# Feed-forward input product in seven block products for eight (Strassen's method), output sums carried by DMA stores that add, in a hybrid encoder block

## Chip, core and metric

The kernel runs on one core of a Trainium2 chip. The metric is the device time of one execution in microseconds (us). Engines are named TensorE (PE in the rows; PEld is its weight load), VectorE (DVE), ScalarE (ACT), GpSimd (POOL) and SyncE (SP, which only issues DMAs).

## The reference

An encoder block on 1024 tokens of width 1024: an attention branch and a state-space branch behind one input projection, mixed by gates, then a SwiGLU feed-forward part. The change lies in the last part, but for eight rows of the conditioning vector `ada`:

```python
ada = jax.nn.silu(c) @ w_ada[l] + b_ada[l]
sh1, sc1, gt1, sh2, sc2, gt2 = jnp.split(ada[:, None, :], 6, axis=-1)
...
h = _rms(x, g_pre_ffn[l]) * (1.0 + sc2) + sh2
g, up = jnp.split(h @ w_ffn_in[l], 2, axis=-1)      # 1024 x 1024 @ 1024 x 5632
f = (jax.nn.silu(g) * up) @ w_ffn_out[l]            # 1024 x 2816 @ 2816 x 1024
x = x + gt2 * _rms(f, g_post_ffn[l])
```

## The kernel before

Everything is float32. A product is made from operands split into a high part that TensorE takes as it is and a low part that is the rest: `mm3` (lines 197 to 203) issues three matmuls for each 128x128 block of weights, high x high, high x low, low x high, on 512 columns of tokens. The split costs a copy on ScalarE and a subtraction on VectorE, for weights in `WStream.split` (line 183 and `tt`, line 66), for activations in the functions that make them.

Tokens are in two halves of 512 columns, named h = 0 and 1 (`halves`). The normalised input of the feed-forward part is `h2t[h]`, eight blocks of 128 rows each. The 2816 hidden columns are 22 pairs of a gate and an up tile of 128 columns. `ffn_in(p, hs)` (line 1599) makes, for one pair and each half, two products of 8 blocks x 3 matmuls, then Silu on ScalarE, the multiply, and the split of f into `fhi` and `flo`. `ffn_out` (line 1616) multiplies the pairs of one group by the output weights: for each m of 8 and each half, 3 matmuls a pair, and VectorE adds the result onto a running sum in SBUF, `facc` (line 1625).

`FGROUPS` (line 33) sets the groups, 4, 4, 4, 4, 3 and 3 pairs, and `units` the order: for each group its input products, then its output products. In the first and the last group the two halves are run one after the other. In the first this lets the second half's normalisation (`chain`) run beside the first half's products; in the last it lets the first half's last pass, `final` (row sums of squares, scaling, the sum with the kept `x1d`, stores), run beside the second half's input products. The second half of the last group goes in two quarters of 256 columns. `backlog`, `tick` and `drain` (line 1463) cut such side work into pieces: `prod` (line 1477) calls `tick` after every second block, which emits the next piece and the stores in `pending` (ScalarE's queue).

All instructions are in program order on each engine; waits are by semaphores. PSUM has eight buffers of 512 columns in this stage (`ps_b`). Weights come by SyncE's queue into two raw buffers of 512 KB (`wraw`) and three split ones (`whi`, `wlo`). The last eight rows of `ada` are loaded and reduced (`ada_do`, line 937) within the feed-forward stage.

## Time and profile before

| | |
|---|---|
| three runs, us | 1680.84, 1685.55, 1686.59; median 1685.55 |
| the profiled execution, us | 1684.47, span of its instructions 1682.7 |
| granted TensorE clock, mean | 0.983 of full speed |
| DMA | 189.66 MB, 113 GB/s over the span |
| feed-forward stage | about 915 us to the end |

Rows of the profile give busy times for each engine, and a row of the trace in order of time says what ended the idle time ahead of an instruction. A matmul's duration is that from its start to the end of its results; the next one starts before.

### The profile page before, as it was taken

Reading aid. Unit: us, or ns where it says so; the run is one execution under the profiler, and the core shown is the slowest. Engines: PE = TensorE matmul, PEld = TensorE weight load, DVE = VectorE, ACT = ScalarE, POOL = GpSimd, SP = SyncE. Lnnn points to the kernel's source line nnn. Section 1 sums busy time; section 2 is a strip of 40 time slices with the busy share of each in tenths; the row PEclk is TensorE's granted clock in tenths of the full one; section 3 lists DMA queues with packets and bytes.
Section 4 is the critical chain, followed back from the end, with each engine's and each line's share of the span. In section 5 each row is a group of like instructions: output and inputs, shape, how many; then the busy total and the mean of one; then the engine's idle time right before and its main releaser. Section 6 shows DMA issues by size and latency. Waiting matters only on the chain.

```text
span 1682.7 us, 19415 instructions
## 1 busy us (share of the span) xinstructions
PE 1618.4 (96%) x7454; PEld 1309.0 (78%) x7454; DVE 977.7 (58%) x1615; ACT 552.5 (33%) x743; POOL 164.0 (10%) x221
## 2 busy tenths in 40 slices
PE   6989999999899999999999999999999999999995
PEld 6878888888688677767777778888888888888874
DVE  6978898977857778854636763223223222323366
ACT  4142322223531467763334443211111121121233
POOL 0430000012220000000524200000000000000002
PEclk9899999999999999999999999999999999999998
DMA  8143333567987424202523442212111111111243
GB/s 330 63 124 100 108 103 94 157 218 221 310 244 223 104 63 101 45 14 67 196 94 107 162 135 91 73 66 79 59 63 51 50 51 50 51 41 48 80 142 129
DMA packets 90748, 189.66 MB, mean 113 GB/s; under 512 B 19992, under 2 KB 36504, under 8 KB 90656
## 3 DMA queue, kind: packets, MB, share of 16 engines
q1 hardware_dynamic: 57920, 120.62, 23.7%
q10 hardware_dynamic: 27104, 49.95, 8.6%
q0 software_dynamic: 5632, 17.86, 3.5%
q8 instruction: 58, 0.95, 0.2%
q14 instruction: 34, 0.28, 0.1%
HBM read 148.61 MB, written 39.78 MB: 112 GB/s over the span
## 4 chain that ended last, share of the span: by engine, by line
PE 65%; DVE 20%; ACT 5%; DMA 4%; issue 4%; ACTq 1%; SPq 0%; DVEq 0%; POOLq 0%
PE mm L203 17%; PE mm L202 17%; PE mm L201 17%; DVE t L66 5%; DVE wlo L66 2%; PE sc L1255 1%; PE sc L1256 1%; PE sc L1257 1%; PE pv L1281 1%; PE pv L1280 1%; PE pv L1282 1%; ACT whi L183 1%; DMA mxd<-mneg 1%; PE mx L1203 1%; DVE s L695 1%
## 5 line engine op out<-in xcount | busy, mean ns | idle before, releaser
L202 PE MATMUL mm<-mh,whi 128*128 128x512 f32 x736 | 289.3, 393 | 4.8 <-DVE mh L74 3.1
L201 PE MATMUL mm<-mh,whi 128*128 128x512 f32 x736 | 289.8, 394 | 0.8 <-ACT mh L1404 0.5
L203 PE MATMUL mm<-mh,wlo 128*128 128x512 f32 x736 | 288.7, 392 | 1.7 <-DVE wlo L66 1.6
L66 DVE TENSOR_TENSOR wlo<-wraw,whi 128x1024 fp32r<-128x1024 f32 (+1 forms) x128 | 155.8, 1235 | 80.2 <-ACT whi L183 80.1
L66 DVE TENSOR_TENSOR silu<-mm,silu 128x512 f32<-128x512 f32 x44 | 30.4, 692 | 277.4 <-PE mm L203 271.2
L183 ACT CAST whi<-wraw 128x1024 fp32r<-128x1024 f32 (+1 forms) x128 | 129.9, 1036 | 149.0 <-PE mm L202 137.0
L202 PEld LDWEIGHTS mm<-mh,whi 128*128 128x128 f32 x736 | 139.2, 189 | 38.2 <-DVE mh L74 6.6
L203 PEld LDWEIGHTS mm<-mh,wlo 128*128 128x128 f32 x736 | 139.2, 189 | 32.9 <-DVE wlo L66 4.3
L201 PEld LDWEIGHTS mm<-mh,whi 128*128 128x128 f32 x736 | 139.2, 189 | 31.1 <-ACT whi L183 0.9
L201 PE MATMUL mm<-hhi,whi 128*128 128x512 f32 x384 | 156.7, 408 | 1.5 <-ACT ev L604 1.5
L202 PE MATMUL mm<-hlo,whi 128*128 128x512 f32 x384 | 152.8, 398 | 1.4 <-DVE hlo L74 1.4
L203 PE MATMUL mm<-hhi,wlo 128*128 128x512 f32 x384 | 153.5, 400 | 0.0
L201 PE MATMUL mm<-fhi,whi 128*128 128x512 f32 x304 | 118.8, 391 | 0.0
L202 PE MATMUL mm<-flo,whi 128*128 128x512 f32 x304 | 118.5, 390 | 0.0
L203 PE MATMUL mm<-fhi,wlo 128*128 128x512 f32 x304 | 118.3, 389 | 0.0
L66 DVE TENSOR_TENSOR mr<-mm,mr 128x512 f32<-128x512 f32 (+1 forms) x88 | 56.3, 641 | 97.1 <-PE mm L203 97.0
L66 DVE TENSOR_TENSOR plo<-p,phi 128x1024 fp32r<-128x1024 f32 x64 | 78.3, 1224 | 40.0 <-ACT phi L1261 39.6
L1613 ACT CAST fhi<-silu 128x512 fp32r<-128x512 f32 x44 | 27.3, 621 | 222.2 <-DVE silu L66 222.2
L201 PEld LDWEIGHTS mm<-hhi,whi 128*128 128x128 f32 x384 | 73.3, 191 | 19.6 <-ACT ev L604 1.9
L202 PEld LDWEIGHTS mm<-hlo,whi 128*128 128x128 f32 x384 | 73.1, 190 | 18.5 <-DVE hlo L74 1.8
L1260 ACT ACTIVATE p<-sc 128x1024 f32<-128x1024 f32 x64 | 65.7, 1026 | 64.5 <-PE sc L1257 64.5
L203 PEld LDWEIGHTS mm<-hhi,wlo 128*128 128x128 f32 x384 | 73.0, 190 | 17.9 <-DVE wlo L66 0.2
(524 smaller groups left out, 2938.7 us busy)
## 6 DMA issues: line engine op xcount, KB each, us to landing
wraw<-in_wfi SPq DMA_DIRECT2D x58, 512.0 KB
wraw<-in_win SPq DMA_DIRECT2D x26, 512.0 KB
wraw<-in_wfo SPq DMA_DIRECT2D x20, 512.0 KB
gdram<-ev ACTq DMA_DIRECT2D x32, 256.0 KB
wada<-in_wada POOLq DMA_DIRECT2D x15, 512.0 KB, 4.3
wraw<-in_wmix SPq DMA_DIRECT2D x10, 512.0 KB
xT<-in_xT SPq DMA_DIRECT2D x8, 512.0 KB
pw<-in_wadk SPq DMA_DIRECT2D x8, 512.0 KB
```

Source lines behind the costliest of these rows:

```text
L66: return self.eng.tensor_tensor(o, a, b, op=op)
L183: A_.copy(hi, t)
L201: PE.matmul(ps, whi[:, c], rhi, start=first, stop=False)
L202: PE.matmul(ps, whi[:, c], rlo, start=False, stop=False)
L203: PE.matmul(ps, wlo[:, c], rhi, start=False, stop=last)
L695: V.tensor_tensor_scan(t[64:P, 511::-1], r[64:P, ::-1], z[i][64:P, ::-1], 0.0, op0=ALU.mult, op1=ALU.add)
L1203: PE.matmul(pieces[j], qt["qhi"][b][0:96, t * P:(t + 1) * P], qt["khi"][b][0:96, halves[j]], start=True, stop=True)
L1255: PE.matmul(ps[:, c], kh[0:97, kc], qh[0:97, c], start=True, stop=False)
L1256: PE.matmul(ps[:, c], kh[0:96, kc], ql[0:96, c], start=False, stop=False)
L1257: PE.matmul(ps[:, c], kl[0:96, kc], qh[0:96, c], start=False, stop=True)
L1260: A_.activation(p, ps, AF.Exp)
L1613: A_.copy(fh[:, c], t)
```

## The change

Groups are now 4, 2, 2, 2, 2, 2, 2, 2 and 4 pairs. Group 0 goes as before, one half of the tokens after the other. For the 18 pairs from the fifth on, `pair7` makes the gate and up tile for all 1024 tokens by Strassen's method in Winograd's form: weights and activations are cut into 2 x 2 blocks (gate and up by halves of the contraction; halves of the contraction by halves of the tokens), and seven products of 4 blocks x 3 matmuls replace eight. Sums of activation blocks, T1 to T4, are made once (`tops_12`, `tops_4`, `tops_3`); sums of weight blocks, S1 to S4, for each pair on GpSimd (class `Blocks`, which also loads the weights by GpSimd's queue and splits them, three blocks ahead). VectorE combines the seven results. In group order, each `ffn_out` result is copied by ScalarE into one of four buffers (`fio`) and sent to DRAM (`fd`): group 0 by a plain store on SyncE's queue, groups 1 to 7 by stores on GpSimd's queue that add to what is there. The last group loads the sums back and adds them on VectorE. The last group no longer runs its input products by halves; for the first half, `final` now adds x on GpSimd in all eight tiles. The last eight rows of `ada` are loaded and reduced in the last steps of attention. The order of the output weights in DRAM follows the groups.

```diff
-FGROUPS = [4, 4, 4, 4, 3, 3]
+FGROUPS = [4, 2, 2, 2, 2, 2, 2, 2, 4]
+AHEAD = 3
...
         if i in ATT_ADA:
-            ada_do(1)
-            ada_load(min(1, len(ada_rest) - 8), gp, "wada", 1)
+            ada_do()
+        if 51 <= i < 62:
+            if len(ada_live) > 1 or i >= 59:
+                ada_do(1)
+            ada_load(1, ap, "wada", 2, SY)
...
+    for hs in ((0,), (1,)):
+        units += [("in", p, hs) for p in range(FGROUPS[0])] + [("out", 0, hs)]
...
+    fd = dram.tile([2, KD, P, HF], F32, name="fd")
...
+    def ft_put(p, c, t):
+        fh, fl = ft[p]
+        A_.copy(fh[:, c], t)
+        tt(fl[:, c], t, fh[:, c].bitcast(F32), ALU.subtract)
...
+        if g == last:
+            r = facc[h][:, m, c0:c0 + n]
+            tt(r, ps, fio.pop(0), ALU.add)
+            return r
+        r = f_tile()
+        A_.copy(r, ps)
+        if g:
+            G.dma_start(fd[h, m], r, accum_op=ALU.add)
         else:
-            tt(r, ps, r, ALU.add)
-        return r
+            SY.dma_start(fd[h, m], r)
...
+        def load(self, n=1):
+            for _ in range(n):
+                if self.loads:
+                    t = wp.tile([P, D], F32, name="wraw", tag="wraw", bufs=2)
+                    src = self.loads.pop(0)
+                    G.dma_start(t.rearrange("p (m c) -> p m c", m=2) if len(src.shape) == 3 else t, src)
+                    self.raw.append(t)
...
+        def split(self, src, out=None):
+            hi, lo = out or self.new(src.shape[1])
+            A_.copy(hi, src)
+            tt(lo, src, hi.bitcast(F32), ALU.subtract)
+            self.done.append((hi, lo))
...
+                    g, u = self.g, self.u = self.raw.pop(0), self.raw.pop(0)
+                    self.split(g[:, lo])
+                    self.s1, self.s2 = half_tile(c2, "xk", NXK), half_tile(c2, "xk", NXK)
+                    G.tensor_tensor(self.s1, u[:, lo], u[:, hi], op=ALU.add)
+                    G.tensor_tensor(self.s2, self.s1, g[:, lo], op=ALU.subtract)
+                    G.tensor_tensor(u[:, lo], g[:, lo], u[:, lo], op=ALU.subtract)
+                elif kind == "S2":
+                    self.split(self.s2)
+                elif kind == "S1":
+                    self.split(self.s1)
+                elif kind == "S3":
+                    self.split(self.u[:, lo])
+                elif kind == "A12":
+                    self.split(self.g[:, hi])
+                    G.tensor_tensor(self.g[:, hi], self.g[:, hi], self.s2, op=ALU.subtract)
+                elif kind == "A22":
+                    self.split(self.u[:, hi])
+                elif kind == "S4":
+                    self.split(self.g[:, hi])
+                    self.load(2)
+                elif kind == "O":
+                    self.split(self.raw[0][:, halves[j % 2]])
+                    if j % 2:
+                        self.raw.pop(0)
+                        self.load()
+                else:
+                    self.split(self.raw.pop(0), self.out() if j == 3 else None)
...
+        def get(self):
+            self.advance(self.got + 1 + self.ahead())
+            self.got += 1
+            return self.done.pop(0)
+
+        def ahead(self):
+
+            return AHEAD if self.got < len(self.seq) - 5 else 2
...
+    def tops_12():
+
+        for nm in ("T1", "T2"):
+            top_new(nm, mhc.tile([P, KD, HF], F32R, name=nm, tag=nm))
+        v, (h0, l0) = mos[1], h2t[0]
+        for j in range(4):
+            t1, t2 = half_tile(c2, "ht"), half_tile(c2, "sq")
+            stt(t1, v[:, j, :], sh2[:, j:j + 1], h0[:, j, :].bitcast(F32), ALU.add, ALU.subtract)
+            yield
+            tt(t1, t1, l0[:, j, :].bitcast(F32), ALU.subtract)
+            yield
+            t_split(t1, "T1", j)
+            yield
+            stt(t2, v[:, 4 + j, :], sh2[:, 4 + j:5 + j], t1, ALU.add, ALU.subtract)
+            yield
+            t_split(t2, "T2", j)
...
+    def tops_3():
+
+        v = mos[1]
+        top_new("T3", row_big(0, F32R))
+        for j in range(4):
+            t = half_tile(c2, "ht")
+            stt(t, v[:, 4 + j, :], dsh[:, j:j + 1], v[:, j, :], ALU.add, ALU.subtract)
+            t_split(t, "T3", j)
...
+    def sprod(ps, w, x):
+        hi, lo = x
+        for k in range(4):
+            mm3(ps, w, hi[:, k, :], lo[:, k, :], k, k == 0, k == 3)
+            if k % 2:
+                tick()
...
+    def pair7(p, prep):
+
+        (h0, l0), (h1, l1) = h2t[0], h2t[1]
+        b11, b21 = ((h0[:, k:k + 4, :], l0[:, k:k + 4, :]) for k in (0, 4))
+        b22 = h1[:, 4:8, :], l1[:, 4:8, :]
+        lo, hi = halves
+
+        def prod7(x):
+            ps = ps_b()
+            sprod(ps, bl.get(), x)
+            return ps
+
+        p1, u2, u3 = half_tile(c2, "ht"), half_tile(c2, "sq"), half_tile(c2, "acc1", 1)
+        gl, uh = half_tile(c2, "acc0", 1), half_tile(c2, "rs", 1)
+        A_.copy(p1, prod7(b11))
+        tt(u2, prod7(tops["T2"]), p1, ALU.add)
+        ps5 = prod7(tops["T1"])
+        prep()
+        tt(u3, prod7(tops["T3"]), u2, ALU.add)
+        tt(uh, ps5, u3, ALU.add)
+        tt(u2, ps5, u2, ALU.add)
+        tt(gl, prod7(b21), p1, ALU.add)
+        A_.activation(gl, gl, AF.Silu)
+        tt(p1, prod7(tops["T4"]), u3, ALU.add)
+        tt(gl, gl, p1, ALU.mult)
+        ft_put(p, lo, gl)
+        tt(u2, prod7(b22), u2, ALU.add)
+        A_.activation(u2, u2, AF.Silu)
+        tt(u2, u2, uh, ALU.mult)
+        ft_put(p, hi, u2)
...
-            if h and (c0 == 0 or m % 2 == 0):
+            if not h or c0 == 0 or m % 2 == 0:
...
+        big_first = g % 2 == 0
+        for n, p in enumerate(range(starts[g], starts[g + 1])):
+            if (n < 2) == big_first:
+                if n % 2 == 0:
+                    ft_big(1, p)
+            else:
+                ft_new(p)
+            pair7(p, drain if p == starts[1] else tick)
+        if g == last:
+            break
+        order = [(m, h) for m in range(KD) for h in range(2)]
+        for m, h in order:
+            if m % 2 == 0 and h == 0:
+                w = bl.get()
+            ffn_out(g, m, h, w, m % 2 * FGROUPS[g])
...
+    for h, c0, n in ((0, 0, HF), (1, 0, QF), (1, QF, QF)):
+        sq = Squares(c2, half_tile(c2, "acc0" if h == 0 else "acc1", 1)[:, 0:n], V)
+        for m in range(3):
+            f_load(h, m, c0, n)
+        for m in range(KD):
+            if h == m % 2 == 0:
+                out_w[m // 2] = bl.get()
+            if m + 3 < KD:
+                f_load(h, m + 3, c0, n)
+            r = ffn_out(last, m, h, out_w[m // 2], m % 2 * FGROUPS[last], c0, n)
+            sq.add(r)
+            A_.activation(r, r, AF.Copy, scale=gg2[:, m:m + 1])
```

What the change does to the order of instructions is shown at three places. First TensorE, where an output stage begins (`mh` are input blocks, `fhi`, `flo` and in some groups `mr` the two parts of f). Before, a group of four pairs, from its last input matmul on, with the waits of each:

```order
L203 MATMUL mm<-mh,wlo 128x512
L201 MATMUL mm<-fhi,whi 128x512 [waits Activation_49]
L202 MATMUL mm<-flo,whi 128x512
L203 MATMUL mm<-fhi,wlo 128x512 [waits DVE_49]
L201 MATMUL mm<-fhi,whi 128x512
L202 MATMUL mm<-flo,whi 128x512
L203 MATMUL mm<-fhi,wlo 128x512
L201 MATMUL mm<-fhi,whi 128x512
L202 MATMUL mm<-flo,whi 128x512
L203 MATMUL mm<-fhi,wlo 128x512
L201 MATMUL mm<-fhi,whi 128x512 [waits Activation_49]
L202 MATMUL mm<-flo,whi 128x512 [waits DVE_49]
```

Now, the group of pairs 6 and 7:

```order
L205 MATMUL mm<-mh,wlo 128x512
L203 MATMUL mm<-mr_9400,whi 128x512 [waits Activation_49]
L204 MATMUL mm<-mr_9400,whi 128x512
L205 MATMUL mm<-mr_9400,wlo 128x512 [waits DVE_49]
L203 MATMUL mm<-mr_9400,whi 128x512 [waits Activation_49]
L204 MATMUL mm<-mr_9400,whi 128x512 [waits DVE_49]
L205 MATMUL mm<-mr_9400,wlo 128x512
L203 MATMUL mm<-mr_9400,whi 128x512
L204 MATMUL mm<-mr_9400,whi 128x512
L205 MATMUL mm<-mr_9400,wlo 128x512
L203 MATMUL mm<-mr_9400,whi 128x512 [waits Activation_49]
L204 MATMUL mm<-mr_9400,whi 128x512 [waits DVE_49]
```

The waits before are for the last pair's first half, made a pair of products earlier; its second half is first read in the second tile, by the 22nd matmul. Now the second tile follows after six matmuls, and the last pair's second half, with the waits for its high and its low part, is read by the tenth and eleventh.

Second GpSimd, in the output stage of group 2; `wraw` is a raw weight buffer, `xk` a sum of weight blocks, `fd` the running sums in DRAM. Before, its queue held in the feed-forward stage eight loads of `ada` rows and the sums of the last pass. Now:

```order
L1688 DMA wraw<-in_wfi 128x1024 [waits DMASW5_49,DMASW3_49,DVE_49]
L1662 DMA fd<-fio 128x512 [waits DMASW6_49,Activation_49]
L1662 DMA fd<-fio 128x512 [waits DMASW7_49,Activation_49]
L1662 DMA fd<-fio 128x512 [waits Activation_49] x2
L1718 TENSOR_TENSOR xk<-wraw 128x512 [waits DMASW5_49]
L1719 TENSOR_TENSOR xk<-xk,wraw 128x512 [waits DMASW4_49,Pool_49]
L1720 TENSOR_TENSOR wraw<-wraw 128x512
L1662 DMA fd<-fio 128x512 [waits Activation_49] x4
L1662 DMA fd<-fio 128x512 [waits DMASW6_49,Activation_49]
L1662 DMA fd<-fio 128x512 [waits DMASW7_49,Activation_49]
```

A weight load, four stores that add, three sums that need the load, and the other stores stand in one queue.

Third ScalarE, between the first and the second quarter of the last half. Before, the squares (`sq`, `acc`) and scalings followed each other:

```order
L1498 ACTIVATE sq<-mr 128x256 [waits DVE_49]
L1708 ACTIVATE mr<-mr,gg_7139 128x256 [waits Activation_49]
L1494 ACTIVATE acc_12347<-mr 128x256 [waits DVE_49,PE_49]
L1708 ACTIVATE mr<-mr,gg_7139 128x256 [waits Activation_49]
L1498 ACTIVATE sq<-mr 128x256 [waits DVE_49]
L1708 ACTIVATE mr<-mr,gg_7139 128x256 [waits Activation_49]
L1498 ACTIVATE sq<-mr 128x256 [waits DVE_49]
L1708 ACTIVATE mr<-mr,gg_7139 128x256 [waits Activation_49]
```

Now:

```order
L149 DMA out_xt<-mh 128x512 [waits DMAHW0_49,Pool_49]
L149 DMA xk<-x1d 128x512 [waits DMAHW2_49]
L149 DMA out_xt<-mh 128x512 [waits DMAHW3_49,Pool_49]
L149 DMA out_xt<-mh 128x512 [waits DMAHW5_49,Pool_49]
L149 DMA out_xt<-mh 128x512 [waits DMAHW6_49,Pool_49]
L1499 ACTIVATE acc_13162<-mh 128x256 [waits DVE_49,PE_49]
L1940 ACTIVATE mh<-mh,gg_7175 128x256 [waits Activation_49]
L1503 ACTIVATE sq<-mh 128x256 [waits DVE_49]
L1940 ACTIVATE mh<-mh,gg_7175 128x256 [waits Activation_49]
```

The first half's last output stores, each waiting for GpSimd, and loads of x stand ahead of the second quarter's first square.

## Rows read from the trace of the kernel before

**Rows 1.** The page's first part: busy us (share of the span) and instructions of each engine.

```profile
PE 1618.4 (96%) x7454; PEld 1309.0 (78%) x7454; DVE 977.7 (58%) x1615; ACT 552.5 (33%) x743; POOL 164.0 (10%) x221
```

**Rows 2.** Stretches: busy us (count) per engine, granted clock, DMA share, GB/s.

```profile
1050.00:1600.00 550.00, 549.63 (x2424) 454.68 (x2423) 168.12 (x218) 103.18 (x137) 3.18 (x6) 1.00 0.18 59
...
1645.00:1666.00 21.00, 17.05 (x137) 16.39 (x135) 17.07 (x48) 14.05 (x32) 2.20 (x3) 1.00 0.39 130
1666.00:1683.00 17.00, 2.21 (x6) 1.43 (x6) 10.12 (x30) 0.00 (x0) 6.49 (x9) 0.51 0.33 109
```

**Rows 3.** Groups by shape, 1050 to 1600 us: count, busy us, mean ns, idle before.

```profile
L201 PE MATMUL mm<-mh,whi 128*128 128x512 f32 x528 | 205.4, 389 | 0.0
...
L66 DVE TENSOR_TENSOR mr<-mm,mr 128x512 f32<-128x512 f32 x68 | 47.0, 691 | 95.3 <-PE mm L203 95.3
...
L1613 ACT CAST fhi<-silu 128x512 fp32r<-128x512 f32 x33 | 20.5, 621 | 185.0 <-DVE silu L66 185.0
L1610 ACT ACTIVATE silu<-mm 128x512 f32<-128x512 f32 x33 | 19.8, 599 | 110.8 <-PE mm L203 110.8
...
L1623 ACT COPY mr<-mm 128x512 f32<-128x512 f32 x6 | 3.5, 587 | 10.0 <-PE mm L203 10.0
```

**Rows 4.** TensorE in order of time, 1641 to 1646 us: start, us, [idle before].

```profile
1641.35 0.39 PE L203 MATMUL mm<-mh,wlo 128*128 128x512 f32 x1
...
1643.24 0.38 PE L201 MATMUL mm<-fhi,wada 128*128 128x256 f32 x1 [0.79 <-ACT fhi L1613]
1643.97 0.38 PE L202 MATMUL mm<-flo,wada 128*128 128x256 f32 x1 [0.34 <-DVE flo L66]
...
1645.38 0.28 PE L201 MATMUL mm<-fhi,mh 128*128 128x256 f32 x1
1645.50 0.28 PE L202 MATMUL mm<-flo,mh 128*128 128x256 f32 x1
```

**Rows 5.** Groups by shape, whole span, GpSimd's passes of 512 columns.

```profile
L1504 POOL TENSOR_TENSOR acc<-acc,sq 128x512 f32<-128x512 f32 x28 | 40.7, 1461 | 103.7 <-ACT sq L1498 93.5 <-issue 10.0
...
L1412 POOL TENSOR_TENSOR mh<-t,mh 128x512 fp32r<-128x512 f32 x16 | 25.2, 1601 | 61.8 <-ACT mh L1404 61.8
```

**Rows 6.** GpSimd in order of time: one issue.

```profile
319.82 0.54 POOL L951 DMA_DIRECT2D er<-in_wada  x1 [1.02 <-DVE t L66]
```

**Rows 7.** DMA issues: count, KB each, us from issue to landing.

```profile
wada<-in_wada POOLq DMA_DIRECT2D x15, 512.0 KB, 4.3
...
er<-in_wada POOLq DMA_DIRECT2D x10, 256.0 KB, 3.7
...
kr<-pdram POOLq DMA_DIRECT2D x1, 512.0 KB, 11.6
...
qhi<-mxd POOLq DMA_DIRECT2D x8, 4.0 KB, 2.8
```

**Rows 8.** Groups by shape, 1645 to 1683 us, ScalarE's passes of 256 columns.

```profile
L1708 ACT ACTIVATE mr<-mr,gg 128x256 f32<-128x256 f32 x16 | 8.2, 510 | 0.5
...
L1498 ACT ACTIVATE sq<-mr 128x256 f32<-128x256 f32 x14 | 5.7, 409 | 3.5 <-DVE mr L66 3.2
```

**Rows 9.** TensorE in order of time, end of the last quarter.

```profile
1663.59 0.28 PE L203 MATMUL mm<-fhi,mh 128*128 128x256 f32 x1
1666.40 0.77 PE L245 MATMUL mm<-ones,acc 128*128 128x1 f32 x3 [2.53 <-DVE acc L1504]
```

**Rows 10.** The output tensor's instructions: ns min/median/max of a store's issue.

```profile
L147 ACTq DMA_DIRECT2D out_xt<-mr x24: 338/344/587, 1628.9 to 1677.7; - x24
```

**Rows 11.** VectorE in order of time, attention's last steps.

```profile
739.24 1.23 DVE L66 TENSOR_TENSOR plo<-p,phi 128x1024 fp32r<-128x1024 f32 x1 [1.57 <-ACT phi L1261]
742.03 1.23 DVE L66 TENSOR_TENSOR plo<-p,phi 128x1024 fp32r<-128x1024 f32 x1 [1.56 <-ACT phi L1261]
...
756.76 1.22 DVE L66 TENSOR_TENSOR rb<-rb,oraw 64x1024 f32<-64x1024 f32 x1
```

**Rows 12.** Groups by shape, whole span: one conditioning row's reduction.

```profile
L455 DVE SCALAR_TENSOR_TENSOR wada<-wada,sil 128x1024 f32<-128x1024 f32 x24 | 29.3, 1220 | 10.0 <-DMA wada<-in_wada 10.0
```

235 lines of the change are left out of this document (142 added, 93 removed).

## Prediction

> **What bounds the kernel now.** I read the busy shares first, then stretches of the feed-forward stage, then single rows at the places that the change touches. TensorE is busy 96% of the span, VectorE 58% [rows 1]. From 1050 to 1600 us, nearly all of the feed-forward stage, TensorE is never idle and runs at the full granted clock, while VectorE, ScalarE and GpSimd have much room [rows 2]. So each matmul that is left out there is worth its spacing, not its duration: the row of the group says 389 ns [rows 3], but matmuls overlap, and 2424 of them in 550 us come every 226.9 ns [rows 2]. Whatever makes TensorE wait in this stage costs in full. After 1666 us TensorE has no more products, and a chain of small steps ends the run [rows 2].
>
> **Matmuls.** 18 pairs of 128 hidden columns had 8 block products each (gate and up, two halves of the tokens, two halves of the contraction) and now have 7, each of 4 x 3 = 12 matmuls. That is 18 x 12 = 216 matmuls of 512 columns less: 216 x 0.2269 = **-49.0 us**. The last group has four pairs for three, so its second half, in two quarters, has 192 matmuls of 256 columns for 144, against 24 of 512 less. With 0.12 us each [rows 4]: 48 x 0.12 - 24 x 0.2269 = **+0.3 us**. The output product keeps its work.
>
> **Load of the other engines.** A group of two pairs now takes TensorE 14 products of 12 and 16 tiles of 6 matmuls, 14 x 2.72 + 16 x 1.36 = 59.9 us. Beside it VectorE has 18 splits and 22 other passes of 512, 40 x 0.69 = 28 us; ScalarE some 44 passes of about 0.6 us, 26 us [rows 3]; GpSimd 8 sums of 1.46 us and 24 DMA issues of 0.54 us, 25 us [rows 5, 6]. None is a bound on average, so I cost this work at nothing, and look at the places where it is in a chain.
>
> **Seams.** Seven times (groups 1 to 7) the output product starts right after the last product of a pair, and that pair's second half of f is only then made: add, Silu, multiply, copy, subtract. The last three steps are seen before: the last product's matmul starts at 1641.35, the next slot is 1641.58, and the matmul that needs the low part starts at 1643.97, 2.39 us on [rows 4]. An add of 0.69 and a Silu of 0.60 come ahead [rows 3], with handovers 3.74 us. In the changed order ten matmuls that need nothing new stand before that matmul (six of the first tile, three and one of the second): 2.27 us. The rest is a stall of 1.47 us, seven times **+10.3 us**. Before, groups of three or four pairs covered it, and only the last unit paid: 0.79 + 0.34 = 1.1 us [rows 4], which goes away, **-1.1 us**, since in the last group the whole first half of the output covers it.
>
> **The stores that add.** No accumulating DMA is in the trace, so the price is bounded. Let L be the time from its issue to its landing. It goes through GpSimd's queue, and four buffers hold the tiles. I follow one output stage, with 0 at its start. GpSimd first issues a weight load that waits for the split of the weights before it, behind the seam's chain up to its copy, 3.05 us, and takes a cast and a subtraction itself, 1.3 us [rows 3]: at 4.4 us. Four accumulates follow it, then three sums that need that load: landing 4.3 us later [rows 7], 8.7, and 3 x 1.46 more, 13.1. The fifth to eighth accumulates are issued at 13.1 to 14.7, every 0.54 us. The twelfth tile's copy waits for the eighth: 14.7 + L, copy 0.59 [rows 3], issue, L again, copy of the sixteenth: done at 15.9 + 2L. Behind it in ScalarE's queue stands the split of the fourth weight block, 1.3 us. TensorE has its output stage until 23.3 us (16 x 1.36 and the seam) and three products that are already split, to 31.5. So it doesn't wait while 15.9 + 2L + 1.3 is below 31.5: **L below 7.1 us is free**; each us beyond costs 2 us a group, 14 in all. Bounds: a plain load of this size from this queue lands in 3.7 us, and the slowest load of this queue takes 11.6 [rows 7]; lower than the plain load I exclude, since the accumulate moves the same bytes and one read more. At 11.6 the stall would be 9.0 a group, 63 us. I take 6.5: the plain 3.7, plus one more dependent round trip, for which I take the 2.8 of a 4 KB load [rows 7]. It is nearer the low end because that row is the same size, queue and engine; the 11.6 us belongs to a load that stood behind two others. So **0 us**, with 0.6 us of L to spare.
>
> The Trainium skill, "Collectives: The Full Stack", section "The bandwidth ceiling: the fold count and why AG ≠ RS ≠ AR", says that a DMA which adds is slower not for the adding but because it reads two sources through one ring. By that an accumulate would cost the plain load's data time twice; an estimate with the page's own halving gives at most 2 x 3.7 = 7.4 us, 0.6 us a group or 4 us more in the sum, 1656, and less if only the moving part doubles. No run here shows it yet.
>
> **The tail.** The first half's last pass (norm, eight multiplies, eight sums with x, eight stores) was hidden under 33 us of input products (3 pairs x 48 matmuls x 0.2269); now it runs beside the two quarters of the second half. Its eight sums have moved to GpSimd at 1.3 to 1.6 us [rows 5], and ScalarE issues its stores in order, each waiting for its sum, ahead of the second quarter's squares. The first sum can start some 11 us into the first quarter, the last ends at 11 + 8 x 1.46 = 22.7, and only then can ScalarE do 16 passes of 0.41 or 0.51 and eight stores of 0.34, 10.1 us [rows 8, 10]: its squares end near 33 us. The second quarter's products end at 23. The row sums come some 10 us after the products, for 2.8 us now (1663.59 to 1666.40) [rows 9]; of this about 2 us are given back, because the 4 us of idle TensorE between 1645 and 1666 [rows 2] lie inside the same time. I take **+5 us**, with 0 (ScalarE's passes fit between the stores) and 10 as ends.
>
> **Attention.** Eight conditioning rows are reduced in its last steps for in the feed-forward stage, where they were hidden. A step takes 2.79 us, and VectorE is idle 1.57 of it [rows 11]; a row's reduction is 1.22 us [rows 12] with two small steps behind it. It fits, but not beside the passes of the softmax's normalisation (three like the one of 1.22 us) [rows 11]: some 3.7 us late, of which the two steps of lag take most. **+2 us**; 0 to 8.
>
> The sums T1 to T4 of the activations, some 40 passes of 0.69 us on VectorE, lie beside 65 us of group 0's products of the second half, and the weight loads that follow the sixteenth accumulate have, by the same clock, some 4 us of lead: nothing. If that cover is gone, rival 3 says what it costs.
>
> **Sum.** The profiled execution took 1684.47 us; it lies 0.06% under the median of the runs shown, 1685.55. 1684.5 - 49.0 + 0.3 + 10.3 - 1.1 + 0 + 5 + 2 = **1652 us**.
>
> **Rivals.**
> 1. *Slow accumulates.* The four buffers drain slower than the stage fills them; ScalarE's copies wait for them, and the next weights' splits behind the copies. For it: the first sums on GpSimd's queue hold half of the accumulates back, and two round trips follow each other. Against: DMA is used little here, 59 GB/s [rows 2]. The other terms leave 32.5 us, 4.6 a group, so L of 9.4 us eats all of it. At 11.6 us: 1652 + 63 = **1715**, slower. With L from 7.1 to 9 the time is 1652 to 1679.
> 2. *GpSimd late.* An accumulate takes twice the issue time of a plain load, 1.08 us, and a sum the 1.60 of its slower row [rows 5]. Issues and sums ahead of the sixteenth copy then add some 3 us to the chain; less the 1.2 us to spare (2 x 0.6 us of L), 1.8 a group: 1652 + 13 = **1665**. Each engine still has room.
> 3. *The saving isn't had*, because split weights or sums come late and TensorE waits once in each pair: 18 x 2.7 = 49, one product's time per pair; **1701**. Against it: the splits run three products ahead, and the changed order has exactly 192 matmuls fewer (216 - 24).
>
> **Chances.** Forecast (1642 to 1662) 0.57; accumulates or GpSimd late by a little, still faster (1662 to 1680) 0.19; about even (within 0.3%, 5 us, what a measurement of this kernel can tell from no change) 0.07; slow accumulates or late weights, slower 0.17. So faster 0.76, same 0.07, slower 0.17. The range: seams at half price and no cost for tail and attention give 1640; above it takes in an L of 9.9 us, 1652 + 2 x 2.8 x 7 = 1691, and a little of what lies beyond: 1640 to 1696.
>
> **What would show it.** Right: TensorE's spacing is still 0.227 us in the products; seven gaps of about 1.5 us at the first tiles of an output stage, ended by the low part of f; accumulates that land within 7 us; no wait of TensorE for a weight split at the fourth product of a group. Wrong: gaps at that fourth product, with ScalarE's copies ended by DMA; a granted clock below full in the stage; row sums of the last quarter within 3 us of its products (tail too dear) or more than 15 us after them.

## The result: 1.0% slower, and where the profile after puts it

The changed kernel takes 1700.86 us (median of 4 runs, 1699.88 to 1703.06) against 1684.82 us before it (4 runs): ratio 1.010, 95% interval 1.008 to 1.012. Forecast were 1652 us, range 1640 to 1696. The profiled executions have spans of 1698.4 and 1682.7 us; the 15.7 us between them are accounted for below.

The page's busy line and three stretches of the profile after (columns as in [rows 2]: us, then busy us and instructions of TensorE, its weight loads, VectorE, ScalarE and GpSimd, granted clock, DMA share, GB/s):

```profile
PE 1595.7 (94%) x7262; PEld 1280.9 (75%) x7262; DVE 1104.0 (65%) x1806; ACT 666.7 (39%) x985; POOL 403.5 (24%) x463
```

```profile
1050.00:1600.00 550.00, 521.23 (x2187) 416.22 (x2187) 259.03 (x353) 206.78 (x361) 222.16 (x235) 0.98 0.51 108
1100.00:1500.00 400.00, 378.11 (x1586) 303.40 (x1585) 177.26 (x243) 151.80 (x267) 167.72 (x181) 0.97 0.55 111
1656.00:1670.00 14.00, 4.94 (x39) 4.50 (x38) 12.85 (x14) 2.44 (x5) 9.76 (x7) 0.77 0.60 194
```

Against [rows 1]: the matmuls that were to go have gone. Against [rows 2]: in the stage where TensorE was never idle and at full clock it now loses 29 us of 550 to idle time and some more to a lower clock, with 2187 matmuls in place of 2424. No other engine is near its limit there, not even GpSimd, which is busy for 40% of the stretch.

TensorE in order of time shows where it is lost. This is one output stage (group of two pairs) from its first matmuls on; a number in brackets is idle time and what ended it:

```profile
1244.11 0.39 PE L203 MATMUL mm<-fhi,whi 128*128 128x512 f32 x1
1244.34 0.39 PE L204 MATMUL mm<-flo,whi 128*128 128x512 f32 x1
1244.56 0.39 PE L205 MATMUL mm<-fhi,wlo 128*128 128x512 f32 x1
1246.73 0.50 PE L203 MATMUL mm<-fhi,whi 128*128 128x512 f32 x1 [1.78 <-ACT fhi L1619]
1247.45 0.80 PE L204 MATMUL mm<-flo,whi 128*128 128x512 f32 x1 [0.23 <-DVE flo L67]
...
1248.47 0.63 PE L203 MATMUL mm<-fhi,whi 128*128 128x512 f32 x1
1248.90 0.63 PE L204 MATMUL mm<-flo,whi 128*128 128x512 f32 x1
1249.33 0.63 PE L205 MATMUL mm<-fhi,wlo 128*128 128x512 f32 x1
1250.69 0.80 PE L203 MATMUL mm<-fhi,whi 128*128 128x512 f32 x1 [0.74 <-ACT fhi L1619]
...
1254.55 0.39 PE L203 MATMUL mm<-fhi,whi 128*128 128x512 f32 x1
1254.78 0.39 PE L204 MATMUL mm<-flo,whi 128*128 128x512 f32 x1
```

There are two gaps, not one: in front of the fourth matmul, the first that reads the last pair's f at all, and in front of the tenth, which reads its second half. Behind the first gap matmuls come every 0.43 us, not every 0.23, until 1254. That is the lower of the clock's two levels, 1.2 for 2.4 GHz: the granted clock of this stretch is 0.51.

```profile
1247.00:1254.00 7.00, 6.04 (x13) 3.88 (x13) 3.59 (x6) 3.03 (x6) 1.74 (x3) 0.51 0.18 51
```

Start to start less 0.2269 us for each matmul, from the first gap until the spacing is 0.23 again, the seven seams cost 5.5, 7.3, 6.3, 6.7, 5.8, 6.9 and 5.9 us, **44.4 us**. Some 13 of them are matmuls without a gap in front, so clock alone.

Why f is late stands in VectorE's rows ahead of that seam (`acc`, `ht`, `sq` are the sums that make f, `wlo` splits of weights):

```profile
1237.53 0.69 DVE L67 TENSOR_TENSOR rs<-mm,acc 128x512 f32<-128x512 f32 x1
1238.14 0.68 DVE L67 TENSOR_TENSOR sq<-mm,sq 128x512 f32<-128x512 f32 x1
1241.50 0.69 DVE L67 TENSOR_TENSOR wlo<-wraw,whi 128x512 fp32r<-128x512 f32 x1 [2.68 <-ACT whi L1702]
1242.11 0.68 DVE L67 TENSOR_TENSOR acc<-mm,ht 128x512 f32<-128x512 f32 x1
1244.00 0.69 DVE L67 TENSOR_TENSOR wlo<-wraw,whi 128x512 fp32r<-128x512 f32 x1 [1.21 <-ACT whi L1702]
1244.61 0.68 DVE L67 TENSOR_TENSOR ht<-mm,acc 128x512 f32<-128x512 f32 x1
1245.33 0.69 DVE L67 TENSOR_TENSOR acc<-acc,ht 128x512 f32<-128x512 f32 x1
```

VectorE stands 2.68 us in front of the split of the group's first output weights, and again 1.21 us, with the sums for f queued behind. ScalarE and GpSimd in order of time say what those weights waited for; the second row is ScalarE's, the others GpSimd's (`fd<-fio` is a store that adds, `xk` a sum of weight blocks):

```profile
1236.62 1.48 POOL L1688 DMA_DIRECT2D wraw<-in_wfo  x2 [1.11 <-issue]
1240.85 0.62 ACT L1702 CAST whi<-wraw 128x512 fp32r<-128x512 f32 x1 [4.68 <-DMA wraw<-in_wfo]
...
1257.58 1.59 POOL L1718 TENSOR_TENSOR xk<-wraw 128x512 f32<-128x512 f32 x1
1259.25 1.62 POOL L1719 TENSOR_TENSOR xk<-xk,wraw 128x512 f32<-128x512 f32 x1
1260.84 1.30 POOL L1720 TENSOR_TENSOR wraw<-wraw 128x512 f32<-128x512 f32 x1
1262.07 3.46 POOL L1662 DMA_DIRECT2D fd<-fio  x4
```

The load is issued 7.5 us ahead of the seam, when the raw buffers come free, and ScalarE's cast of what it brings starts 4.2 us later. In the output stage, four adding stores stand behind three sums. The groups by shape from 1100 to 1580 us, and the landing times:

```profile
L1662 POOL DMA_DIRECT2D fd<-fio x112 | 96.3, 981 | 58.5 <-ACT fio L1660 55.7 <-ACT whi L1702 2.7
L67 DVE TENSOR_TENSOR wlo<-wraw,whi 128x512 fp32r<-128x512 f32 x103 | 91.7, 891 | 126.9 <-ACT whi L1702 124.8
L1660 ACT COPY fio<-mm 128x512 f32<-128x512 f32 x112 | 65.7, 587 | 111.2 <-DMA fd<-fio 83.2 <-PE mm L205 27.9
```

```profile
fd<-fio POOLq DMA_DIRECT2D x112, 256.0 KB, 5.3
wraw<-in_wfi POOLq DMA_DIRECT2D x36, 512.0 KB, 4.1
```

An adding store lands in 5.3 us, inside what the prediction called free, but its issue takes 0.98 us of GpSimd for the 0.54 of [rows 6], and ScalarE waits 83 us for the buffers in seven groups, with the next weights' splits behind it. TensorE's waits for split weights in the same stretch (for `whi`) come to 1.2 us, against 22.5 us for f.

### The profile page after: what moved, and what is told of

Read it like the earlier page. It is cut to its first block, busy times and chain, and to the rows that moved or that the text cites. A ratio compares the mean times of both kernels' runs of the same rounds, so it can differ in the third digit from the quotient of the medians.

```text
span 1698.4 us, 19977 instructions
## 1 busy us (share of the span) xinstructions
PE 1595.7 (94%) x7262; PEld 1280.9 (75%) x7262; DVE 1104.0 (65%) x1806; ACT 666.7 (39%) x985; POOL 403.5 (24%) x463
## 4 chain that ended last, share of the span: by engine, by line
PE 37%; DVE 28%; issue 11%; ACT 9%; POOL 7%; DMA 7%; SPq 1%; ACTq 0%; DVEq 0%; POOLq 0%
PE mm L205 7%; PE mm L204 7%; PE mm L203 6%; DVE t L67 5%; DVE wlo L67 5%; DVE sq L67 2%; ACT whi L1702 2%; DMA wraw<-in_wfo 2%; PE mm L1398 1%; PE sc L1256 1%; PE sc L1257 1%; ACT whi L185 1%; PE sc L1258 1%; POOL fd L1662 1%; PE pv L1282 1%
## 5 line engine op out<-in xcount | busy, mean ns | idle before, releaser
L67 DVE TENSOR_TENSOR wlo<-wraw,whi 128x512 fp32r<-128x512 f32 (+2 forms) x191 | 196.0, 1031 | 195.2 <-ACT whi L1702 138.2
L204 PE MATMUL mm<-mh,whi 128*128 128x512 f32 x448 | 176.0, 393 | 4.9 <-DVE mh L75 2.9
L205 PE MATMUL mm<-mh,wlo 128*128 128x512 f32 x448 | 176.3, 394 | 3.0 <-DVE wlo L67 2.9
L203 PE MATMUL mm<-mh,whi 128*128 128x512 f32 x448 | 176.9, 395 | 0.8 <-ACT mh L1408 0.5
L1660 ACT COPY fio<-mm 128x512 f32<-128x512 f32 x128 | 75.0, 586 | 120.7 <-DMA fd<-fio 83.2
L1702 ACT CAST whi<-wraw 128x512 fp32r<-128x512 f32 (+1 forms) x121 | 74.4, 631 | 111.8 <-DMA wraw<-in_wfi 44.2
L1662 POOL DMA_DIRECT2D fd<-fio x112 | 96.3, 981 | 58.5 <-ACT fio L1660 55.7
L203 PE MATMUL mm<-mr,whi 128*128 128x512 f32 (+1 forms) x236 | 94.3, 400 | 14.0 <-ACT mr L1619 11.5
L204 PEld LDWEIGHTS mm<-mh,whi 128*128 128x128 f32 x448 | 84.5, 189 | 26.9 <-DVE mh L75 6.3
L203 PEld LDWEIGHTS mm<-mh,whi 128*128 128x128 f32 x448 | 84.5, 189 | 19.9 <-ACT whi L185 1.3
L204 PE MATMUL mm<-mr,whi 128*128 128x512 f32 (+1 forms) x236 | 92.9, 394 | 2.1 <-DVE mr L67 2.1
L205 PE MATMUL mm<-mr,wlo 128*128 128x512 f32 (+1 forms) x236 | 92.4, 391 | 0.3
L203 PE MATMUL mm<-fhi,whi 128*128 128x512 f32 (+1 forms) x196 | 78.0, 398 | 13.4 <-ACT fhi L1619 13.4
```

The source lines that it names most:

```text
L67: return self.eng.tensor_tensor(o, a, b, op=op)
L203: PE.matmul(ps, whi[:, c], rhi, start=first, stop=False)
L204: PE.matmul(ps, whi[:, c], rlo, start=False, stop=False)
L205: PE.matmul(ps, wlo[:, c], rhi, start=False, stop=last)
L1660: A_.copy(r, ps)
L1662: G.dma_start(fd[h, m], r, accum_op=ALU.add)
```

## Experiments

Four theories. **A**: the seam is the bare chain from the last product to f, and the clock behind the gap. **B**: the adding stores and GpSimd set the pace. **C**: one late load, whose split blocks VectorE, moves the chain of f. **D**, formed after the first eight runs: the late load is the end of a loop that runs once per group, from the split of the last output weights through load, GpSimd's sums, adding stores queued behind them, ScalarE's copies, and the next splits behind the copies. Ratios are to the kernel before on the same chip. Its medians on the chips used lie between 1681.1 and 1685.5 us, so a difference of medians between two rows can be off by some 4 us; where that matters, the difference by the ratios stands beside it.

| run | us | ratio (95%) | seven seams, us | load ahead of seam, us |
|---|---|---|---|---|
| the change | 1700.9 | 1.010 (1.008 to 1.012) | 44.4 | 7.2 to 8.5 |
| e1_korder | 1694.0 | 1.006 (1.004 to 1.009) | 32.7 | 7.2 to 7.9 |
| e2_ufirst | 1706.9 | 1.014 (1.011 to 1.017) | 48.6 | 7.2 to 7.6 |
| e3_plain | 1685.2 | 1.001 (1.000 to 1.003) | 25.7 | 7.2, then 10.2 to 10.4 |
| e4_sync | 1696.4 | 1.008 (1.005 to 1.010) | 32.5 | 7.6 to 8.4 |
| e5_hold | 1723.0 | 1.024 (1.022 to 1.027) | 15.4 | |
| e6_filler | 1693.1 | 1.008 (1.006 to 1.011) | | |
| e7_hold_korder | 1725.3 | 1.026 (1.024 to 1.028) | | |
| e8_tailv | 1706.4 | 1.015 (1.012 to 1.017) | 43.3 | |
| e9_vsums | 1687.2 | 1.004 (1.002 to 1.006) | 34.9 | 7.5 to 9.7 |
| e10_groups4 | 1677.6 | 0.998 (0.996 to 1.000) | 15.8 in four | 7.2 to 10.2 |
| e11_vsums_sync | 1680.4 | 0.999 (0.997 to 1.001) | 27.1 | 7.8 to 10.0 |
| e12_g4_all | 1667.6 | 0.992 (0.990 to 0.994) | 11.3 in four | 7.8 to 9.9 |
| e13_vs_korder | 1675.7 | 0.996 (0.993 to 0.998) | 15.7 | 7.8 to 9.3 |
| e14_g4_korder | 1664.8 | 0.989 (0.985 to 0.993) | none in four | |
| e15_tailqueue | 1662.8 | 0.989 (0.985 to 0.992) | none in four | |

The last column is the time from the issue of a group's first output-weight load to the first matmul of its output stage, read off both queues' rows.

### More cover: e1_korder

```diff
-        order = [(m, h) for m in range(KD) for h in range(2)]
-        for m, h in order:
...
-            ffn_out(g, m, h, w, m % 2 * FGROUPS[g])
+        order = [(m, h) for h in range(2) for m in (j, j + 1)]
...
+        for k in range(2):
+            for m, h in order:
...
+                mm3(pss[m, h], w, tiles[k][0][:, c], tiles[k][1][:, c], m % 2 * 2 + k, k == 0, k == 1)
```

> Groups 1 to 7 make their output product four tiles at a time: the three matmuls of the first pair for all four tiles, then those of the second pair, first half of the tokens first. The same matmuls, but the second pair's f is first read by the 13th matmul for the 4th, and its second half by the 19th for the 10th. The changed kernel lost 44.4 us at its seven output stages (6.3 each), at gaps in front of the 4th and the 10th matmul and in matmuls of 0.43 us spacing behind them. Theory A (the bare chain from the last product to f, plus the lower clock that follows a gap): nine matmuls, 2.04 us, of more cover take away the first gap (some 1.9 us) and most of the second, and with them the slow matmuls: 1.0 to 2.5 us a seam are left, 1664 to 1675 us. Theory B (accumulating stores or GpSimd set the pace of a group): the gaps come back elsewhere in the group, 1695 to 1702. Theory C (a weight split that waits for a late load blocks VectorE, and the whole chain of f moves with it): the first gap goes, the second stays at 1 us or more with slow matmuls, 1672 to 1685.

11.7 us of the seams went, not the 27 or more of A, and the time lies in none of the three ranges. With nine matmuls more of cover, the gap in front of the second half stayed at 1.8 us, because f was no earlier. A alone falls.

### The load one product earlier: e2_ufirst

```diff
-                self.loads += [a["wfi"][2 * i], a["wfi"][2 * i + 1]]
+                self.loads += [a["wfi"][2 * i + 1], a["wfi"][2 * i]]
...
                 elif kind == "A22":
                     self.split(self.u[:, hi])
+                    self.load()
```

> The up tile of the weights is loaded ahead of the gate tile, and the next load is issued as soon as the up tile has been split for the last time, one product (2.7 us) earlier than now, where both loads wait for the gate tile's last split. So the first output weights of a group land some 2.7 us earlier. Theory C (VectorE stands 2.68 us in front of the split of the first output block, whose load lands late, with the sums for f behind it): the first gap of each seam goes (1.9 us), the second shrinks to the 1.5 us of the bare chain, some slow matmuls stay: 2 to 4 us a seam less, 1673 to 1688. Theory A (bare chain and clock): VectorE's wait is only in the shadow of the products, 1697 to 1702. Theory B (stores that add): 1697 to 1702.

A miss for all three, and the edit didn't do what it was meant to: VectorE makes the splits of a pair's sixth and seventh block right behind each other, so both buffers come free within 1 us and both loads are still issued as one pair (1372.09, for a seam at 1379). They come no earlier than in the changed kernel, 7.2 to 7.6 us ahead of the seam for 7.2 to 8.5, so the run doesn't test C.

### The adding taken away: e3_plain

```diff
-            G.dma_start(fd[h, m], r, accum_op=ALU.add)
+            SY.dma_start(fd[h, m], r)
```

> The stores of groups 1 to 7 are plain ones on SyncE's queue instead of ones that add on GpSimd's; the sum over the groups is left out, the rest is the same. Theory B (the adding stores, their issue on GpSimd, or the queue that they share with the weight loads set the pace): 20 us or more faster, 1660 to 1680. Theories A and C: the seam doesn't depend on them, 1695 to 1702; ScalarE's waits in front of its copies of the output tiles (83 us now) go without the time following.

B has a part: 16 us (14 by the ratios), between the ranges of B and of the others, and the seams fall to 25.7. The edit takes away the adding, GpSimd's issues and the shared queue together, so it doesn't say which of them counts. Loads now come 10.3 us ahead of six of the seven seams; at the first it is still 7.2, and that seam still has two gaps and costs 7.1 us. In the groups by shape ScalarE's copies wait for TensorE alone, and in the waits VectorE waits 39.6 us for TensorE in that stretch, in the changed kernel 4.0: there it ran late through whole groups. The other six seams have one gap, before the tenth matmul, and VectorE's rows show it:

```profile
1297.74 0.69 DVE L67 TENSOR_TENSOR mr<-acc,mr 128x512 fp32r<-128x512 f32 x1 [0.69 <-ACT mr L1619]
1298.35 0.68 DVE L67 TENSOR_TENSOR wlo<-wraw,whi 128x512 fp32r<-128x512 f32 x1
1298.95 0.68 DVE L67 TENSOR_TENSOR sq<-mm,sq 128x512 f32<-128x512 f32 x1
1300.34 0.69 DVE L67 TENSOR_TENSOR sq<-sq,rs 128x512 f32<-128x512 f32 x1 [0.70 <-ACT sq L1848]
1301.71 0.69 DVE L67 TENSOR_TENSOR mr<-sq,mr 128x512 fp32r<-128x512 f32 x1 [0.69 <-ACT mr L1619]
```

The last product's last matmul starts at 1297.69. Its sum (`sq<-mm,sq`) starts at 1298.95 because the first half's low part and a weight split stand ahead of it. That seam costs 2.4 us and keeps the clock; every second one of the six costs 3.8 to 4.1 and has slow matmuls.

### Loads on another queue: e4_sync

```diff
-                    G.dma_start(t.rearrange("p (m c) -> p m c", m=2) if len(src.shape) == 3 else t, src)
+                    SY.dma_start(t.rearrange("p (m c) -> p m c", m=2) if len(src.shape) == 3 else t, src)
```

> The weight loads of the 18 Strassen pairs and of the output stages behind them are issued by SyncE's queue for GpSimd's, so that they no longer stand among the adding stores and GpSimd's sums, and their issue (some 0.55 us, and some 1.1 us from the releasing split to it) is SyncE's. Theory C: a load lands 0.5 to 1 us earlier, the wait of VectorE at each seam is shorter by as much: 1693 to 1699. Theory A: no change, 1698 to 1702. Theory B: loads no longer held by the stores, 1670 to 1690.

In time this is in C's range, but its interval overlaps the changed kernel's. The seams lose 12 us less; VectorE's wait in front of the first output split is 1.7 us for 2.7.

### The splits held back: e5_hold and e7_hold_korder

```diff
-            self.advance(self.got + 1 + self.ahead())
+            while self.n < len(self.seq):
+                kind, _, j = self.seq[self.n]
+                if self.n - self.got > (k if kind != "O" else 1 if j == 1 else 2):
+                    break
+                self.advance(self.n + 1)
```

> The splits of a group's first two output weight blocks are issued later: the first one product ahead of now behind the last pair's fourth sum (two products ahead for three), the second behind the last pair's second half of f. So ScalarE and VectorE no longer stand in front of a load that has not landed with the sums for f behind it. Theory C (head-of-line wait for the late load; VectorE waits 2.68 and 1.21 us there in the changed kernel): the first half of f comes 3 us earlier, its gap goes; the second half is left with the bare chain's 1.4 us and a lower clock behind it, 3.3 us a seam for 6.3: 1676 to 1684. Theory B (the lag comes from the stores that add and runs through the whole group): VectorE is as late as before, 1694 to 1702. Theory A (bare chain and clock): 1697 to 1702.

> The held splits of e5_hold and the order of e1_korder (first pair's matmuls of four tiles ahead of the second pair's). Theory C with the bare chain: the second half of f is read by the 19th matmul, 4.1 us behind the last product, and its chain takes 3.7: nearly no gap, no lower clock, under 1 us a seam for 6.3: 1660 to 1670. Theory B: the gaps of e1_korder (4.7 us a seam) stay for the larger part, 1682 to 1694.

At the seam C was right: 15.4 us in place of 44.4. But the kernel lost 22 us (24 by the ratios), for a reason that none of the three names. TensorE's waits in e5, 1100 to 1580 us (total, times, longest):

```profile
PE mm L203 <- ACT whi L1702: 22.6, 10, 3.9
PE mm L203 <- ACT fio L1660: 9.1, 8, 1.9
PE mm L203 <- ACT fhi L1619: 4.6, 4, 1.2
```

And GpSimd's rows in one of its groups:

```profile
1253.55 0.56 POOL L1688 DMA_DIRECT2D wraw<-in_wfi  x1 [11.01 <-DVE wlo L67]
...
1264.80 1.28 POOL L1718 TENSOR_TENSOR xk<-wraw 128x512 f32<-128x512 f32 x1 [5.90 <-DMA wraw<-in_wfi]
...
1268.65 3.47 POOL L1662 DMA_DIRECT2D fd<-fio  x4
```

A split made later frees its raw buffer later: the next pair's load is issued 12.5 us behind the output weights' load, in the changed kernel 8.4 (1236.62 to 1245.00). The sums wait for it, four stores wait behind the sums, the copies for the stores (108 us for 83 in the stretch), and TensorE now for split weights and free PSUM buffers. More cover (e7) takes nearly all of the gaps at the seams away, and the time is no better for it. This suggests that the queues form a loop, and that what one step of it gives up comes back at the next: theory D.

### The clock: e6_filler

```diff
+                if k == 0:
+                    fill(w, tiles[0][0][:, 0:HF], 8 if h == 0 else 0)
+                if k == 1:
+                    fill(w, tiles[0][0][:, 0:HF], 6 if h == 0 else 0)
```

> The changed kernel with matmuls whose result nobody reads in the two gaps of each seam: 8 in front of the 4th and 6 in front of the 10th matmul of an output stage, 3.2 us of the 3.9 to 5.5 us that TensorE idles there. All else waits as before. Clock theory: TensorE's spacing of 0.43 us behind the gaps comes from the gaps; with them filled the granted clock stays full, and the slow part of each seam (1.6 to 2.8 us, 13 us in all, and some of the matmuls between the gaps) goes: 1684 to 1692. If the lower clock has another cause, or costs nothing because TensorE would have waited for f anyway: 1698 to 1704.

98 matmuls more, and 7.7 us less by the medians; by the ratios it is 3 us, and the intervals overlap. Between the two marks shown under "Why the prediction was wrong", the profiled executions take 731.3 us for 736.9. The granted clock of the stretch is full again:

```profile
1100.00:1500.00 400.00, 393.16 (x1695) 316.73 (x1695) 171.46 (x245) 151.72 (x266) 166.92 (x182) 1.00 0.57 113
```

So the lower clock comes from the gaps. Filling them is worth some 6 us in the stage, not all 13, which fits that part of the slow matmuls only filled the time in which the second half of f was awaited anyway. As a difference of whole times it is not clear of noise.

### The loop cut: e9, e11

```diff
-                    G.tensor_tensor(self.s1, u[:, lo], u[:, hi], op=ALU.add)
-                    G.tensor_tensor(self.s2, self.s1, g[:, lo], op=ALU.subtract)
+                    tt(self.s1, u[:, lo], u[:, hi], ALU.add)
+                    tt(self.s2, self.s1, g[:, lo], ALU.subtract)
...
```

> The four sums of weight blocks per pair are made by VectorE (0.69 us each) for GpSimd (1.3 to 1.6 us), so GpSimd's queue holds only weight loads and the stores that add. Theory D (once per group a loop runs through the queues: split of the last output weights, load, GpSimd's sums, the adding stores queued behind those sums, ScalarE's copies that wait for the stores' buffers, the next splits behind the copies; the late loads at the seam are its end): one link is cut, stores no longer wait for a weight load's sums, VectorE is 2 to 3 us less late at the seam, 15 to 25 us in all: 1676 to 1688. Theory C alone (only the load in front of the seam's splits is late, for its own reasons): VectorE has 2.8 us a pair more to do and the gap stays: 1699 to 1708.

> As e9, and the weight loads issued by SyncE: GpSimd's queue holds nothing in groups 1 to 7 but the stores that add. Theory D: no link of the loop is left but the four buffers (copy, issue, landing); between e9 and the plain stores of e3 (1685): 1672 to 1684. Theory C alone: 1695 to 1704.

Both in D's ranges, as far as times go: 14 and 20 us less by the medians, 9 and 18 by the ratios, though the same stores add the same bytes, and VectorE has 2.8 us a pair more to do. From the second seam on, loads move to 9 or 10 us ahead of it, as with plain stores. But e9 doesn't isolate D's link from sums to stores: ScalarE's waits for the stores' buffers only fall from 83 to 70 us, while two other things change with it (groups by shape, 1100 to 1580 us). VectorE's splits of raw weights get shorter, 70.9 us in all for 91.7, and ScalarE no longer waits for GpSimd's sums, 37 us in the changed kernel, but for VectorE's, 16. Which of these makes the loads earlier is not told apart. That the loads' place among the stores costs something is shown by e11 against e9: the same edit as in e4, on one chip, and the intervals don't touch.

### Fewer seams, more cover: e10, e12, e13, e14

```diff
-FGROUPS = [4, 2, 2, 2, 2, 2, 2, 2, 4]
+FGROUPS = [4, 4, 4, 4, 2, 4]
...
```

In groups of four pairs the output weights are also split 1024 columns at a time, for 512.

> Groups of 4, 4, 4, 4, 2 and 4 pairs for 4, seven times 2, and 4: the same products, four output stages that add for seven, 64 adding stores for 112, and in the first three of them 2.7 us of TensorE work a tile for 1.36, so the four buffers drain in time; the last pair's f is read by the 10th and the 22nd matmul for the 4th and the 10th. Theory D: three of four seams nearly go (under 1.5 us), the one of the group of two pairs stays at 5 to 7: some 34 us less, 1662 to 1672. Theory C alone: each seam keeps a gap of 1 to 2 us and the slow matmuls behind it, 3 to 4 us in four places: 1670 to 1678. If the weight path between pairs is the limit rather than the seam (a load every 20 us where TensorE needs 19), it shows now as gaps in front of products: 1680 to 1695.

> e10 and e11 together. Theory D: the group of two pairs loses less as well, and the loads land earlier: 1655 to 1667. Theory C alone: 1670 to 1680.

> e11 (sums on VectorE, loads on SyncE) with the order of e1: the second pair's f is read by the 13th and the 19th matmul of an output stage for the 4th and the 10th. In e11 the seams still lose 27 us, 2.3 to 6.1 each. If what is left there is the bare chain from the last product to f, and the lower clock that follows a gap (theory A as the remainder behind theory D): 2.0 us of cover end nearly all of it, under 1 us a seam: 1657 to 1664. If loads are still late there: as in e1, a quarter of it: 1672 to 1680.

> e12 with that order in all its four output stages: the first three pairs' matmuls of four tiles (36, 8.2 us) ahead of the last pair's. e12's seams lose 11.3 us in four places. Theory A as the remainder: 9 to 11 us less, 1656 to 1660; the four buffers for the output tiles now fill in a burst of four in 2.7 us every 10.9 us, which could hold ScalarE for a few us without TensorE's waiting. If late loads are the remainder: 1663 to 1668.

e10 fell into C's range, not D's, and its rows speak against D as the whole cause: ScalarE waits only 11.9 us for the stores' buffers, so that link hardly holds, and still the four seams cost 2.8 to 4.9 us. At the dearest the load is issued 7.2 us ahead, and VectorE stands 3.25 us in front of the split of what it brings, with the sums for f behind it, as in the changed kernel. What makes the load late there is not shown. e12, with the sums on VectorE and the loads on SyncE as well, came out 0.6 us above D's range. e13 and e14 ask what is left once loads are early, and A as the remainder fails in e13: 2.2 us a seam stay, with loads 7.8 to 9.3 us ahead. Its rows show why: from the last product's end (1298.6 in one seam) to the high part of f (1304.4) pass 5.8 us, not 3.7, since two weight splits and the sums and the low part of the first half stand ahead on VectorE. In e14, where the last pair's f is first read by the 37th matmul (in the group of two by the 13th), all four seams are gone, and the stretch is without idle time and at full clock, as before the change:

```profile
1100.00:1500.00 400.00, 399.93 (x1744) 326.74 (x1743) 204.12 (x304) 139.24 (x235) 52.31 (x60) 1.00 0.41 91
```

By its time e14 is not told apart from e12 (intervals 0.985 to 0.993 and 0.990 to 0.994); the seams are told apart by the rows. It missed the 1656 to 1660 us that the end of the seams was to give: about 5 of the 11 us came back in front of the last group's first tile, which costs 6.2 us in e14 and 0.8 in e12.

### The tail: e8_tailv, e15_tailqueue

```diff
-            if not h or c0 == 0 or m % 2 == 0:
+            if h and (c0 == 0 or m % 2 == 0):
```

> Only the tail: the first half's eight sums with x in the last pass are VectorE's again, as before the change. In the changed kernel TensorE waits 9.06 us for the first quarter's row sums while VectorE's passes last 1.26 us for 0.7 and 1.47 us for 0.42 beside GpSimd's sums. If GpSimd's sums cause this (they lengthen VectorE's passes, and ScalarE's stores wait for them): 4 to 9 us faster, 1692 to 1697. If the tail is bound by the sheer number of passes that used to lie under input products: 0 to 3 us, 1698 to 1701.

```diff
-                later(xs[m], x1d[m][:, c])
+                G.dma_start(xs[m], x1d[m][:, c])
...
-            later(out[m][:, c], r)
+            (G.dma_start if not h else later)(out[m][:, c], r)
```

> e14, and in the first half's last pass the eight stores of the output and the eight loads of x go by GpSimd's queue, behind GpSimd's own sums, for ScalarE's queue. In the changed kernel ScalarE stands 11.1 us in front of the second quarter's first square while it issues stores that each wait for a sum of GpSimd. If this in-order issue is the tail's cost: the second quarter's squares start up to 10 us earlier, 5 to 9 us less than e14. If VectorE's passes are (they come last in front of the row sums), 0 to 2 us less, or a few us more by GpSimd's issues.

e8 is slower by some 5 us (8 by the ratios), a miss for both readings: the wait for the first quarter's row sums grows from 9.1 to 13.1 us, although VectorE's passes are short again. e15 is the same as e14 within the interval. So neither GpSimd's sums nor ScalarE's order of issue is the tail's cost by itself. What the rows of the changed kernel show is VectorE, 12.85 of the 14 us busy from 1656 to 1670, with eight multiplies that used to lie under input products:

```profile
1662.09 6.29 DVE L67 TENSOR_TENSOR mh<-mh,rs 128x512 f32<-128x512 f32 x5
1668.30 1.48 DVE L1509 TENSOR_TENSOR acc<-acc,sq 128x256 f32<-128x256 f32 x1
```

That VectorE's passes are the tail's limit is argued from this and from e8, and not shown by a run that takes them away.

## Why the prediction was wrong

The marks in TensorE's rows, first of the kernel before, then of the changed one: the row sums ahead of the feed-forward stage, the first matmul of 256 columns, and, after, the last product and the last row sums (before: 1666.40 [rows 9]).

```profile
906.18 0.95 PE L245 MATMUL mm<-ones,acc 128*128 128x1 f32 x8
1641.58 0.28 PE L201 MATMUL mm<-fhi,wada 128*128 128x256 f32 x1
```

```profile
907.38 0.84 PE L247 MATMUL mm<-ones,acc 128*128 128x1 f32 x7
1644.29 0.28 PE L203 MATMUL mm<-mr,whi 128*128 128x256 f32 x1
1683.01 0.28 PE L205 MATMUL mm<-fhi,mh 128*128 128x256 f32 x1
1685.07 0.61 PE L247 MATMUL mm<-ones,acc 128*128 128x1 f32 x4 [1.78 <-DVE acc L1509]
```

| step | predicted, us | measured, us |
|---|---|---|
| matmuls, with the quarters | -48.7 | -48.8 |
| seams | +10.3 | +44.4 |
| rest of the stage | 0 | +11.6 |
| accumulates, in themselves | 0 | in the seams |
| tail, with the old seam that was to go | +5 - 1.1 | +7.3 |
| attention | +2 | +1.2 |
| sum | -32.5 | +15.7 |

**Matmuls: right.** Between the first two marks 240 matmuls of 512 columns fewer (216, and 24 that moved into the quarters) are 54.5 us at the spacing of [rows 2]; the quarters have 48 more, 5.7 us. Where nothing waits the spacing is still 0.23 us. The mark moved by only +1.5 us (735.4 us between them before, 736.9 now), so 56.0 were lost there: 44.4 at seams and 11.6 elsewhere. Of the latter, gaps at the last output tiles of group 0 and at the last group's weights and first tile are the largest; about 3 us I did not locate. The old seam of 1.1 us lies behind the mark and did go, but the last group's first tile now costs 3.2 us for the same reason as the seven: its f is late. The prediction had the whole first half of the output cover it.

**Seams: wrong, and this is the step that failed.** The count (seven) and the place of the second gap, at the last pair's second half of f, were right; the price was 6.3 us for 1.47. Three things were missing. The step took ten matmuls as needing nothing new; the first half of f, read by the fourth, was taken as there, and it came 2 us late. The chain of 3.74 us was laid out as if VectorE were free for it. In the changed kernel it stands in front of splits whose weights are not there, 2.68 and 1.21 us in the rows above, with the sums for f behind; even with plain stores a low part and a weight split stand ahead of the last sum, 0.85 us, and the cheapest seams cost 2.3 (e3). And the lower clock behind a gap was priced at nothing; it is 13 us in the rows, of which e6 gave back some 6.

**The stores that add: L was right, the test was too short.** L came out at 5.3 us for the 6.5 taken and the 7.1 called free, and at the next products TensorE indeed waits for almost no weights. But the step asked only whether TensorE's next products have their weights. By theory D, ScalarE, GpSimd and VectorE were all late by then and stayed late, since each split waits for a load, each load for a split, and all of it runs in program order; the bill came two pairs later, at the next seam. That the stores have such a part is shown by e3, that GpSimd's sums and the shared queue have one by e9 and e11; which link holds the load back is open, and e10 shows a late load almost without waits for the stores. The count of GpSimd's issues for a group was off as well, 24 for 22 (sixteen stores, six loads); nothing hung on it. Rival 2 had the right piece, an issue of 0.98 us, and too small a price, 13 us, at the wrong place. Of rival 1 the cause is out: L came to 6.9 us at most, not 9.4. But its chain, copies that wait for the four buffers with the next splits behind them, is what the 83 us of ScalarE's waits are. Rival 3 gave 1701, which is the time that was measured, by a mechanism that isn't there: it has TensorE wait once in each of 18 pairs, and the rows show the waits at seven seams, for f.

The estimate that the prediction worked out by the Trainium skill, "Collectives: The Full Stack", section "The bandwidth ceiling: the fold count and why AG ≠ RS ≠ AR", gave up to 7.4 us for a DMA that adds; the trace has 5.3 for 256 KB beside 4.1 for a plain load of 512 KB from that queue, dearer than plain and under the estimate. It changed nothing in the result.

**Tail and attention: inside their bounds.** From the first matmul of 256 columns to the last row sums 40.8 us, before 24.8; less the 5.7 of matmuls that is +10.3, and from there to the end 13.3 for 16.3, -3.0. So the size was about right, but not the way to it. The row sums were to come some 10 us after the products; they come 2 us after them (1683.01 to 1685.07), because the products themselves stop for 9 us for the first quarter's row sums, which the step did not have. That the size came near is in part luck. The stage begins 1.2 us later than before.

**What would show it.** The list named gaps of 1.5 us ended by the low part of f; they are ended by the high part, and there are two. A granted clock below full in the stage was named as a sign of being wrong, and was one. Row sums within 3 us of the last quarter's products were to mean a tail priced too dear; they came at 2 us, with a tail that was not.

The change itself is sound: with the loop cut and more cover at the seam, the same seven block products for eight give 1664.8 and 1662.8 us, 1.1% under the kernel before. That is 11 to 13 us short of the forecast, although no seam is left. In e14 gaps and slow matmuls still cost 17 us in the quarters and 10 at group 0's last tiles and the last group's first.
